# A TensorE order written out by hand for an attention stage, and a tail that transposes over all score banks

## The chip, the cores and the metric

One core of one Trainium2 chip. The metric is the device time of one launch in microseconds (us). The engines that matter here: TensorE (PE, with its weight loads PEld), VectorE (DVE), ScalarE (ACT), GpSimd (POOL), and SyncE (SP), whose queue issues most DMAs.

## What is computed

Two layers of a mixer block over 2048 latent and 256 context tokens, width 1024. Each layer projects its normed input into four branches (attention, convolution, Fourier mixing, spatial gating), gates them and projects them back. The change concerns the attention of each layer and the norm at the end of the convolution branch, which runs beside it. All in float32:

```python
def _attend(q, k, v):                       # 4 heads, 64+32 wide
    scale = 1.0 / math.sqrt(QK_NOPE + QK_ROPE)
    s = jnp.einsum("bqhd,bkhd->bhqk", q, k) * scale
    pr = jax.nn.softmax(s, axis=-1)
    return jnp.einsum("bhqk,bkhd->bqhd", pr, v)

# latent queries read 2048 + 256 keys; context queries (layer 0 only) read 256 keys
# convolution branch: y = silu(layernorm(depthwise_conv(glu)))   then a 256x256 product
# layer: x = x + gate * (concat(attn, conv, four, sgu) * silu(gates)) @ w_out
```

## The kernel before

The kernel is written for a planner: code is emitted in program order, the planner puts each engine's instructions into one fixed order by priority (program order) and by what it reckons to be ready, assigns buffers from pools of a fixed count, and places every wait. So the order on TensorE is fixed before the run, but by the planner and not by the program text.

A layer has three stages: projections (phase A), attention, and the output projection. Attention runs over two **pairs** of heads (`attention`). A pair runs over **jobs** of 256 queries: 8 latent jobs of 18 key tiles each and, in layer 0, one context job of 2 key tiles in second place. A job has four **steps** j (2 heads x 128 queries). The work of a step:

- **Scores** (`score_steps`): five PSUM banks of 512, 512, 512, 512 and 256 keys. A bank is three matmuls (`mm3`, a hi/lo split: L286 to L288). VectorE takes each bank's maximum (L1008), then the row's maximum (L1012); only then ScalarE turns the five banks into `e` tiles by exp (L1017). The pool `s` has 5 banks, so a step's first bank is free again when the step before has had its first exp.
- **Key tiles** of the job before (`av_steps`): four transposes of `e` into a bank of the pool `t` (L1038, 2 banks), copied to `et` by DVE (L1041, letter v) or ACT (L1043, letter a).
- **Products with V** (L1031): two heads, each written once in the code and run as two instructions, so four instructions a key tile, into the one bank `o`. In the code they come two key tiles at a time, at least three behind the transposes (`LAG`, `GRP`).
- **Reciprocals**: four diagonal tiles (POOL L1077), broadcast by matmuls into a `t` bank (L1054), copied by ACT (L1057), multiplied by DVE (L1061) and stored (L1062).
- **Convolution** (`side`): two taps on DVE (L1459) and one half of a norm step (`Conv.tail`): first two transposes of `cac` into a `t` bank (L1492), DVE statistics (L1494), a power on POOL (L292) and the normed tile (L1499); in the next call two transposes back (L1503) and two copies (L1505). There are 18 such tiles in layer 0 and 16 in layer 1.

`PLAN` is the program order of a step: s is a score bank, v or a a key tile. After it comes one `side()`. The last job's key tiles are emitted alone at the end (the **tail**), v and a in turn. Before attention a tiny exp is emitted so that ACT has its table (L1321). K1 (`k1p`) holds the keys of the second pair, loaded in the second job (`half`).

Of the kernel before, what the change touches and what calls it, by code (L numbers as in the profile page):

```python
# [24 lines left out]
P = 128  # L25
# [173 lines left out]
class Kern:  # L199
    def __init__(self, tc, A, outT):  # L200
        self.tc = tc
        self.nc = tc.nc
        self.A = A
        self.outT = outT
        self.n = 0
        self.pse = self.np = self.ap = None
        self.cnt, self.dq, self.every, self.conv = 0, [], None, None
        self.lastp = False


    def nm(self, s):
# [63 lines left out]
    def split(self, src, hi, lo):  # L275
# [2 lines left out]
        b = self.nc.vector.tensor_tensor(lo, src, hi.bitcast(F32), op=ALU.subtract)  # L278
        return a.ins, b.ins

    def mm3(self, out, ks, start=True, stop=True):

        n = len(ks)
        mm = self.nc.tensor.matmul
# [734 lines left out]
        job.es.append(es)  # L1019
        yield  # L1020

    def av_steps(self, p, vt, job):

        nc = self.nc
        dgs = job.dgs

        def product(kt, et):
            g = job.k0 // P + kt
            for q in range(2):
                h = 2 * job.p + q  # L1030
                nc.tensor.matmul(job.o[64 * q:64 * q + 64, 0:256], lhsT=vt[:, g, 64 * h:64 * h + 64],  # L1031
                                 rhs=et[:, 256 * q:256 * q + 256], start=kt == 0, stop=kt == job.nk - 1)

        pend = []
        for kt in range(job.nk):
            ps = self.bank("t")
            for j in range(4):
                nc.tensor.transpose(ps[:, j * P:(j + 1) * P], job.es[j][kt], self.ident)  # L1038
# [5 lines left out]
            if kt == 0:  # L1044
                job.o = self.bank("o")
            pend.append((kt, et))
            if len(pend) >= LAG + GRP:
                for _ in range(GRP):
                    product(*pend.pop(0))
            if kt == min(RBK, job.nk - 1):  # L1050
                rb = self.bank("t")
                for j in (0, 2, 1, 3):
                    q, t = j // 2, j % 2
                    nc.tensor.matmul(rb[64 * q:64 * q + 64, t * P:(t + 1) * P], lhsT=self.ones[:, :64], rhs=dgs[j],  # L1054
                                     start=True, stop=True)
                rs = self.x("co", 256)
                nc.scalar.copy(out=rs, in_=rb[:, 0:256])  # L1057
            if kt == job.nk - 1:
                for e in pend:
                    product(*e)  # L1060
                nc.vector.tensor_tensor(rs, job.o[:, 0:256], rs, op=ALU.mult)  # L1061
                nc.gpsimd.dma_start(out=job.S["att"][job.p * P:(job.p + 1) * P, job.q0:job.q0 + 256], in_=rs)  # L1062
            yield 1


    PLAN = ["vsssssvav", "vassasssvv"]

    def av_queue(self, p, vt):

        nc, job = self.nc, self.avw  # L1070
        rs = self.st()
        nc.vector.reduce_sum(rs[:, 0:4], job.sm[:, :, :5 if job.k0 == 0 else 1], axis=AX.X)
        nc.vector.reciprocal(rs[:, 4:8], rs[:, 0:4])
        job.dgs = []
        for j in range(4):
            dg = self.dg()
            nc.gpsimd.tensor_scalar(dg, self.ident, rs[:, 4 + j:5 + j], None, op0=ALU.mult)  # L1077
            job.dgs.append(dg)
        self.avq.append(self.av_steps(p, vt, job))

    def av_go(self, n=None):

        while self.avq and (n is None or n > 0):
            if next(self.avq[0], None) is None:
                self.avq.pop(0)
            elif n is not None:
                n -= 1

    def attention(self, l, S, p, vt, qpool, pr, keys, side, half, first=None):
# [8 lines left out]
        ahead = list(first or [])  # L1098
        for i, q0 in enumerate(qs):
            job = Job()  # L1100
            job.p, job.q0, job.S = pr, q0, S
            job.k0, klen = (0, NTOK) if q0 < T else (T, C)
            job.nk = klen // P
            job.es, job.sm = [], self.t(p, "sm", [P, 4, 5], bufs=3)
            if i == 0 and not first:
                ahead = [load(0), load(1)]
            qq = ahead.pop(0)
            if i > 0 and i + 1 < len(qs):
                ahead.append(load(i + 1))
            if i == 1:  # L1110
                half()
            for j in range(4):
                sc = self.score_steps(p, job, keys[j // 2], qq[j // 2], (j % 2) * P,
                                      list(FB[j]) if first and i == 0 else [])
                for c in self.PLAN[j % 2] if q0 < T else ("vs", "as")[j % 2]:
                    if c == "s":
                        next(sc, None)
                    else:
                        self.evac = c
                        self.av_go(1)  # L1120
                if not first or i > 0:
                    side()
# [132 lines left out]
    def build(self):  # L1255
        tc, nc, A = self.tc, self.nc, self.A
        with ExitStack() as es:
# [37 lines left out]
            for l in range(L):  # L1295
# [11 lines left out]
                with self.pool(f"V{l}", "right") as vp:  # L1307
# [14 lines left out]
                    with self.pool(f"B{l}", "right") as p, self.pool(f"K1_{l}", "right") as k1p:  # L1322
                        tail = conv.tail(k1p)
                        next(tail)

                        def side():
                            with tc.issue_after(self.red.ins):
                                conv.pump(LATE)
                            return next(tail, True)

                        kn = []
                        self.avq, self.avw, self.ep = [], None, k1p
                        self.attention(l, S, p, vt, k0p, 0, keys, side, lambda: kn.extend(self.load_keys(S, k1p, 1)), [q0, q1])
# [5 lines left out]
                        self.attention(l, S, p, vt, vp, 1, kn, side, lambda: None)  # L1339
                        while not side():  # L1340
                            pass
                        self.av_queue(p, vt)
                        while self.avq:
                            self.av_go(1)
# [7 lines left out]
                with self.pool(f"O{l}", "right") as p, self.pool(f"G{l}", "right") as gp:  # L1352
                    if last:
                        self.np = p
                    blocks = list(range(0, T, 256)) + ([] if last else [T])
                    wpw = self.load_wpw(l, gp, wop)
                    ys = self.out_load(l, 0, S, wpw, gp, wop, ORD1)
                    ws += self.load_wo(l, gp, range(4, 8), wop)
                    for i, t0 in enumerate(blocks):
                        nxt = []  # L1360

                        def ahead():
                            if i + 1 < len(blocks):
                                nxt.extend(self.out_load(l, blocks[i + 1], S, wpw, gp, (p, wop)[i % 2], OUT_ORDER))
# [8 lines left out]
                        self.tick()  # L1373
                    if not last:
                        S = self.scratch(l + 1)
                wo.__exit__(None, None, None)
            self.pse.close()

# [5 lines left out]
class Conv:  # L1384
# [76 lines left out]
    def tail(self, pool):  # L1461
# [19 lines left out]
        for t0 in range(0, end, w):  # L1481
# [6 lines left out]
            for t in range(w // P):  # L1488
                sl = slice(t * P, (t + 1) * P)
                ps = k.bank("t")  # L1490
                for c in range(2):
                    nc.tensor.transpose(ps[:, c * P:(c + 1) * P], acc[c][:, sl], k.ident)  # L1492
# [7 lines left out]
                yield  # L1500
                tr = k.bank("t")
                for c in range(2):
                    nc.tensor.transpose(tr[:, c * P:(c + 1) * P], yn[:, c * P:(c + 1) * P], k.ident)  # L1503
# [20 lines left out]
```

## Time and profile before

| | us |
|---|---|
| median of three runs (2925.22 to 2936.71) | 2926.96 |
| the profiled execution | 2933.03 |
| its span on the core | 2931.3 |
| attention of layer 0, first score to last product with V | 747.8 to 1314.3 |
| attention of layer 1 | 2167.6 to 2711.1 |

The span holds 1.7 us less than the execution, and the profiled execution is 6.1 us above the median of the runs. In a timeline the columns are start, duration, engine, line, operation, tiles and shape, and the count of equal instructions in a row. A matmul's duration includes its pipeline, so what an instruction costs TensorE is read from one start to the next.

### The profile page before, as it was taken

To read this page: it belongs to the slowest core of one execution; us is meant where nothing else is said; L and a number is where in the kernel's file an instruction comes from. 1 tells how busy PE (TensorE), PEld (TensorE's weight loads), DVE (VectorE), ACT (ScalarE), POOL (GpSimd) and SP (SyncE) were. 2 spreads that over 40 slices of the span, in tenths; PEclk is the share of its full clock that TensorE was granted. 3 is DMA by queue.
4 is the path that set the end of the run, shared out by engine and by line. 5 is a ranking of instruction groups with operands and counts; after the bars stand their busy time and mean duration, and the time that the engine had idled before them with its cause. 6 is when DMAs were issued, how large, how long until landed. Compare 5 with 4: busy or idle time off the path is not lost. (4 is left out here: it accounts for less than half of the span.)

```text
span 2931.3 us, 50512 instructions
## 1 busy us (share of the span) xinstructions
PE 2826.8 (96%) x18434; PEld 2425.8 (83%) x18434; DVE 1958.5 (67%) x4301; ACT 1207.0 (41%) x3228; POOL 549.8 (19%) x901
## 2 busy tenths in 40 slices
PE   6999999999899999999999999999989999999998
PEld 4889999999667766769998899998776777776998
DVE  4578498485477777654444695894837777775554
ACT  3432343433344555543223343343434455554432
POOL 1311311421111011012322113114301100111210
PEclk9999999999899999999999999999999999999999
DMA  7465343434611010016543543443543101000653
GB/s 247 138 200 177 107 135 108 144 128 130 182 45 33 25 51 23 21 35 211 178 156 126 164 153 104 135 135 128 172 160 91 35 21 46 17 28 24 183 154 112
DMA packets 222745, 326.75 MB, mean 111 GB/s; under 512 B 33456, under 2 KB 153264, under 8 KB 221728
## 3 DMA queue, kind: packets, MB, share of 16 engines
q1 hardware_dynamic: 194368, 245.51, 27.8%
q0 software_dynamic: 27696, 77.98, 7.7%
q8 instruction: 145, 2.38, 0.4%
q14 instruction: 104, 0.85, 0.1%
q10 hardware_dynamic: 432, 0.04, 0.0%
HBM read 232.30 MB, written 91.10 MB: 110 GB/s over the span
## 5 line engine op out<-in xcount | busy, mean ns | idle before, releaser
L286 PE MATMUL mm<-hh,ring 128*128 128x384 f32 (+1 forms) x1408 | 489.6, 348 | 0.0
L288 PE MATMUL mm<-hh,ring 128*128 128x384 f32 (+1 forms) x1408 | 483.1, 343 | 1.8 <-DVE ring L278 1.7
L1017 ACT ACTIVATE e<-s,st 128x512 f32<-128x512 f32 (+1 forms) x636 | 400.1, 647 | 203.8 <-DVE st L1012 191.6
L1008 DVE TENSOR_REDUCE st<-s 128x1 f32<-128x512 f32 (+1 forms) x636 | 384.0, 630 | 148.8 <-PE s L288 146.7
L287 PE MATMUL mm<-hl,ring 128*128 128x384 f32 (+1 forms) x1408 | 483.2, 343 | 0.0
L1459 DVE SCALAR_TENSOR_TENSOR acc<-win,c_cw,acc 128x384 f32<-128x384 f32 (+5 forms) x780 | 426.9, 570 | 7.5
L1038 PE MATMUL t<-ident,e 128*128 128x128 f32 x2320 | 344.0, 279 | 3.9 <-DVE et L1041 2.6
L1031 PE MATMUL o<-et,v 128*64 128x256 f32 x2320 | 344.6, 392 | 0.0
L1038 PEld LDWEIGHTS t<-ident,e 128*128 128x128 f32 x2320 | 261.5, 142 | 96.4 <-issue 42.4
L1041 DVE COPY et<-t 128x512 f32<-128x512 f32 x377 | 257.9, 686 | 97.5 <-PE t L1038 90.2
L286 PE MATMUL mm<-yh,woh 128*128 128x256 f32 x1040 | 296.9, 285 | 5.6 <-ACT woh L277 3.1
L287 PE MATMUL mm<-yl,woh 128*128 128x256 f32 x1040 | 293.8, 283 | 0.0
L288 PE MATMUL mm<-yh,wol 128*128 128x256 f32 x1040 | 293.4, 282 | 0.2 <-DVE wol L278 0.2
L277 ACT CAST ring<-wst 128x256 fp32r<-128x256 f32 (+2 forms) x480 | 183.5, 418 | 262.2 <-DMA wst<-winC 158.1
L286 PEld LDWEIGHTS mm<-hh,ring 128*128 128x128 f32 x1408 | 266.0, 189 | 19.3 <-issue 9.9
L288 PEld LDWEIGHTS mm<-hh,ring 128*128 128x128 f32 x1408 | 266.1, 189 | 8.6 <-DVE ring L278 2.8
L287 PEld LDWEIGHTS mm<-hl,ring 128*128 128x128 f32 x1408 | 266.3, 189 | 5.9
L1043 ACT COPY et<-t 128x512 f32<-128x512 f32 x203 | 119.2, 588 | 331.2 <-PE t L1038 330.7
L278 DVE TENSOR_TENSOR ring<-wst,ring 128x256 fp32r<-128x256 f32 (+2 forms) x480 | 199.9, 449 | 83.4 <-ACT ring L277 76.9
L1031 PEld LDWEIGHTS o<-et,v 128*64 128x64 f32 x2320 | 153.1, 136 | 98.9 <-issue 52.4
L286 PEld LDWEIGHTS mm<-yh,woh 128*128 128x128 f32 x1040 | 198.3, 191 | 7.1 <-ACT woh L277 3.5
L287 PEld LDWEIGHTS mm<-yl,woh 128*128 128x128 f32 x1040 | 198.3, 191 | 0.3 <-DVE yl L278 0.3
(310 smaller groups left out, 5265.1 us busy)
## 6 DMA issues: line engine op xcount, KB each, us to landing
wst<-winC SPq DMA_DIRECT2D x192, 256.0 KB, 3.1
ast<-wada SPq DMA_DIRECT2D x32, 512.0 KB, 4.7
gt<-g SPq DMA_DIRECT2D x102, 128.0 KB, 3.0
g<-co POOLq DMA_DIRECT2D x60, 192.0 KB, 2.5
wst<-winB SPq DMA_DIRECT2D x24, 384.0 KB, 3.7
x<-xn POOLq DMA_DIRECT2D x72, 128.0 KB, 2.7
ast<-wada SPq DMA_DIRECT2D x8, 1024.0 KB, 8.7
fst<-ft SPq DMA_DIRECT2D x32, 256.0 KB, 3.3
```

Source lines behind the costliest of these rows:

```text
L277: a = self.nc.scalar.copy(out=hi, in_=src)
L278: b = self.nc.vector.tensor_tensor(lo, src, hi.bitcast(F32), op=ALU.subtract)
L286: mm(out, lhsT=lh, rhs=rh, start=start and i == 0, stop=False)
L287: mm(out, lhsT=lh, rhs=rl, start=False, stop=False)
L288: self.last = mm(out, lhsT=ll, rhs=rh, start=False, stop=stop and i == n - 1)
L1008: self.red = nc.vector.reduce_max(mx[:, i:i + 1], ps[:, :w], axis=AX.X)
L1017: nc.scalar.activation(out=e, in_=ps, func=AF.Exp, bias=nb[:, 0:1], accum_out=sm[:, i:i + 1])
L1031: nc.tensor.matmul(job.o[64 * q:64 * q + 64, 0:256], lhsT=vt[:, g, 64 * h:64 * h + 64], rhs=et[:, 256 * q:256 * q + 256], start=kt == 0, s ...
L1038: nc.tensor.transpose(ps[:, j * P:(j + 1) * P], job.es[j][kt], self.ident)
L1041: nc.vector.tensor_copy(et, ps)
L1043: nc.scalar.copy(out=et, in_=ps)
L1459: eng.scalar_tensor_tensor(ac, win[:, t:t + w], v["cw"][:, l, c, t:t + 1], ac, op0=ALU.mult, op1=ALU.add)
```

## The change

- `behind` and `whole` chain every TensorE instruction of attention to the one before it in program order (an edge without a semaphore): scores, key tiles, products, reciprocals and the convolution's transposes. The planner can no longer reorder them.
- A step is now `vnbvsasasss` (j even) or `vnbvsasasass` (j odd): key tile, convolution step (n), **burst** (b), key tile, then score banks and key tiles in turn. A context step is `vnbvs`.
- `av_burst` issues all products of the waiting key tiles but the last one (`LAG` 1), of one job at a time, and behind a job's last key tile the reciprocals, which go into the free half of bank `o`.
- ACT copies 5 of 9 key tiles where it copied 3 of 9.
- Buffers: `e` 21 and 10 for 23 and 9, `et` 8 for 5. Room for them comes from the first block's `y` tiles, which get a pool of their own after attention (`yp`).
- Keys of the second pair are loaded in the fourth job, its first queries in the last job but one.
- Tail: four key tiles (v, a, v, a), then a burst; transposes take turns over one `t` and two `s` pools' banks (`"tsstss"`). A tiny Silu is emitted ahead of it, for ACT's table.

```diff
-EB, EB2, LAG, GRP, ETB, RBK = 23, 9, 3, 2, 5, 4
+EB, EB2, LAG, ETB = 21, 10, 1, 8
+    def whole(self, r):
+        if self.chain is not None:
+            if self.chain:
+                self.behind(r.ins, self.chain[0])
+            self.chain = [r.ins]
+        return r
...
+    def av_burst(self, vt, lag=LAG):
+        nc = self.nc
+        todo = [e for e in self.pend[:max(0, len(self.pend) - lag)] if e[0] is self.pend[0][0]]
+        if not todo:
+            return
+        self.pend = self.pend[len(todo):]
+        job = todo[0][0]
+        if todo[0][1] == 0:
+            job.o = self.bank("o")
+        for _, kt, et in todo:
+            g = job.k0 // P + kt
+            for q in range(2):
+                h = 2 * job.p + q
+                self.whole(nc.tensor.matmul(job.o[64 * q:64 * q + 64, 0:256], lhsT=vt[:, g, 64 * h:64 * h + 64],
+                                            rhs=et[:, 256 * q:256 * q + 256], start=kt == 0, stop=kt == job.nk - 1))
+        if kt < job.nk - 1:
+            return
+        for j in (0, 2, 1, 3):
+            q, t = j // 2, j % 2
+            dg = self.dg()
+            nc.gpsimd.tensor_scalar(dg, self.ident, job.inv[:, 4 + j:5 + j], None, op0=ALU.mult)
+            self.whole(nc.tensor.matmul(job.o[64 * q:64 * q + 64, 256 + t * P:256 + (t + 1) * P], lhsT=self.ones[:, :64],
+                                        rhs=dg, start=True, stop=True))
...
-    PLAN = ["vsssssvav", "vassasssvv"]
+    PLAN = ["vnbvsasasss", "vnbvsasasass"]
...
-                for c in self.PLAN[j % 2] if q0 < T else ("vs", "as")[j % 2]:
+                for c in self.PLAN[j % 2] if q0 < T else "vnbvs":
                     if c == "s":
                         next(sc, None)
+                    elif c == "b":
+                        self.av_burst(vt)
+                    elif c == "n":
+                        if not first or i > 0:
+                            side()
...
+                        nc.scalar.activation(out=self.st()[:, 0:1], in_=self.mhalf[:, 0:1], func=AF.Silu)
+                        self.tb = "tsstss"
                         while self.avq:
-                            self.av_go(1)
-                            self.evac = "v" if self.evac == "a" else "a"
+                            for c in "vava":
+                                self.evac = c
+                                self.av_go()
+                            self.av_burst(vt)
+                        while self.pend:
+                            self.av_burst(vt, 0)
```

## Rows read from the trace of the kernel before

**Rows 1.** The page's first part: busy us and share of each engine.
```profile
PE 2826.8 (96%) x18434; PEld 2425.8 (83%) x18434; DVE 1958.5 (67%) x4301; ACT 1207.0 (41%) x3228; POOL 549.8 (19%) x901
```
**Rows 2.** Windows: both attentions, then a tail; length, busy by engine, PEclk, DMA share.
```profile
747.00:1314.00 567.00, 553.12 (x3542) 395.07 (x3540) 400.56 (x846) 281.17 (x789) 66.02 (x115) 0.98 0.17 49
...
2167.00:2711.00 544.00, 534.23 (x3460) 383.83 (x3458) 395.62 (x818) 274.81 (x769) 56.87 (x98) 0.99 0.16 47
...
1299.00:1313.00 14.00, 14.00 (x112) 9.20 (x111) 4.15 (x6) 4.44 (x9) 0.00 (x0) 1.00 0.05 13
```
**Rows 3.** Timeline, PE: the first and the last run of products with V.
```profile
782.55 1.51 PE L1031 MATMUL o<-et,v 128*64 128x256 f32 x10
...
2709.14 1.95 PE L1031 MATMUL o<-et,v 128*64 128x256 f32 x16
```
**Rows 4.** Timeline, PE, layer 0: key tiles among scores, then among products.
```profile
838.12 0.60 PE L1038 MATMUL t<-ident,e 128*128 128x128 f32 x4
838.47 0.48 PE L288 MATMUL s<-k1h,ql 96*128 96x512 f32 x1
838.79 0.39 PE L286 MATMUL s<-k1h,qh 96*128 96x512 f32 x1
...
841.06 1.08 PE L1031 MATMUL o<-et,v 128*64 128x256 f32 x8
842.08 0.66 PE L1038 MATMUL t<-ident,e 128*128 128x128 f32 x4
842.66 0.65 PE L1031 MATMUL o<-et,v 128*64 128x256 f32 x2
843.24 0.66 PE L1038 MATMUL t<-ident,e 128*128 128x128 f32 x4
843.83 1.08 PE L1031 MATMUL o<-et,v 128*64 128x256 f32 x6
844.83 0.44 PE L1492 MATMUL t<-ident,cac 128*128 128x128 f32 x2
```
**Rows 5.** Timeline, PE, layer 1: a long run of products, a convolution transpose behind it.
```profile
2337.05 1.95 PE L1031 MATMUL o<-et,v 128*64 128x256 f32 x16
2338.93 0.44 PE L1492 MATMUL t<-ident,cac 128*128 128x128 f32 x2
2339.20 0.60 PE L1038 MATMUL t<-ident,e 128*128 128x128 f32 x4
```
**Rows 6.** The chain in order of time: the same run in successive jobs (start, us).
```profile
2302.93 1.88 PE o L1031 x16
2337.12 1.88 PE o L1031 x16
...
2498.40 1.88 PE o L1031 x16
2529.77 1.88 PE o L1031 x16
```
**Rows 7.** Timeline, layer 0: first instruction behind a step's scores; the step's first exp.
```profile
1276.36 0.60 PE L1038 MATMUL t<-ident,e 128*128 128x128 f32 x4
...
1277.92 0.69 ACT L1017 ACTIVATE e<-s,st 128x512 f32<-128x512 f32 x1 [2.55 <-DVE st L1012]
```
**Rows 8.** Timeline, layer 1: a convolution tile's transposes, and its normed tile on DVE.
```profile
2677.33 0.38 PE L1492 MATMUL t<-ident,cac 128*128 128x128 f32 x2
...
2679.84 0.54 DVE L1499 TENSOR_SCALAR yn<-t,st,st 128x256 f32<-128x256 f32 x1
```
**Rows 9.** Groups by line, attention of layer 0: key tiles copied by DVE and ACT.
```profile
L1041 DVE COPY et<-t 128x512 f32<-128x512 f32 x189 | 129.1, 686 | 54.1 <-PE t L1038 51.7 <-ACT et L1043 1.9
...
L1043 ACT COPY et<-t 128x512 f32<-128x512 f32 x103 | 60.4, 588 | 166.1 <-PE t L1038 165.9
```
**Rows 10.** Timeline, PE: the first convolution transpose of layer 0 and its wait.
```profile
773.35 0.47 PE L1492 MATMUL t<-ident,cac 128*128 128x128 f32 x1 [0.45 <-DMA cac<-dw]
```
**Rows 11.** The line of the early exp: engine, count, durations in ns, first and last start.
```profile
L1321 ACT ACT_TABLE_LOAD  x2: 1283/1283/1283, 632.9 to 2085.1; - x2
```

More of the change, by code (lines that the diff above doesn't have):

```diff
@@ L208, in __init__ @@
         self.lastp = False
+        self.chain = None
     def nm(self, s):
@@ L279, in split, with behind, mm @@
         return a.ins, b.ins
+    def behind(self, ins, prev):
+        self.tc.add_manual_dep(ins, prev.name, mybir.DependencyInfo(mybir.DependencyClass.NoSync, mybir.DependencyReason.DATA),
+                               reason="order of TensorE")
+    def whole(self, r):
[4 more added lines that the diff above has]
+        return r
     def mm3(self, out, ks, start=True, stop=True):
         n = len(ks)
-        mm = self.nc.tensor.matmul
+        def mm(*a, **kw):
+            return self.whole(self.nc.tensor.matmul(*a, **kw))
         for i, (lh, ll, rh, rl) in enumerate(ks):
@@ L1020, in score_steps, with av_steps @@
         yield
-    def av_steps(self, p, vt, job):
+    def av_steps(self, p, job):
         nc = self.nc
[L1025 to L1034, printed above, removed]
         for kt in range(job.nk):
-            ps = self.bank("t")
+            self.tb = self.tb[1:] + self.tb[:1]
+            ps = self.bank(self.tb[0])
             for j in range(4):
-                nc.tensor.transpose(ps[:, j * P:(j + 1) * P], job.es[j][kt], self.ident)
+                self.whole(nc.tensor.transpose(ps[:, j * P:(j + 1) * P], job.es[j][kt], self.ident))
             et = self.t(self.ep, "et", [P, 512], bufs=ETB)
@@ L1043, in av_steps @@
                 nc.scalar.copy(out=et, in_=ps)
[L1044 to L1062, printed above, removed]
-            yield 1
-    PLAN = ["vsssssvav", "vassasssvv"]
+            self.pend.append((job, kt, et))
+            yield 1
+    def av_burst(self, vt, lag=LAG):
[21 more added lines that the diff above has]
+                                        rhs=dg, start=True, stop=True))
+        rs = self.x("co", 256)
+        nc.scalar.copy(out=rs, in_=job.o[:, 256:512])
+        nc.vector.tensor_tensor(rs, job.o[:, 0:256], rs, op=ALU.mult)
+        nc.gpsimd.dma_start(out=job.S["att"][job.p * P:(job.p + 1) * P, job.q0:job.q0 + 256], in_=rs)
@@ L1068, in av_queue @@
+    PLAN = ["vnbvsasasss", "vnbvsasasass"]
     def av_queue(self, p, vt):
         nc, job = self.nc, self.avw
[L1071 to L1089, printed above, removed]
+        job.inv = self.st()
+        nc.vector.reduce_sum(job.inv[:, 0:4], job.sm[:, :, :5 if job.k0 == 0 else 1], axis=AX.X)
+        nc.vector.reciprocal(job.inv[:, 4:8], job.inv[:, 0:4])
+        self.avq.append(self.av_steps(p, job))
@@ L1091, in attention, with av_go @@
+    def av_go(self):
+        while self.avq and next(self.avq[0], None) is None:
+            self.avq.pop(0)
+    def attention(self, l, S, p, vt, qpool, pr, keys, side, half, first=None, pre=None):
         qs = list(range(0, T, 256))
@@ L1096, in load @@
             return [self.load_q(S, qpool, 2 * pr + q, qs[i]) for q in range(2)]
-        ahead = list(first or [])
+        ahead = list(first or pre)
         for i, q0 in enumerate(qs):
@@ L1104, in attention @@
             job.es, job.sm = [], self.t(p, "sm", [P, 4, 5], bufs=3)
-            if i == 0 and not first:
-                ahead = [load(0), load(1)]
             qq = ahead.pop(0)
-            if i > 0 and i + 1 < len(qs):
+            if (i > 0 or not first) and i + 1 < len(qs):
                 ahead.append(load(i + 1))
-            if i == 1:
-                half()
+            if i == len(qs) - 2:
+                half(1)
+            if i == 3:
+                half(0)
             for j in range(4):
@@ L1331, in build, with half @@
                         kn = []
-                        self.avq, self.avw, self.ep = [], None, k1p
-                        self.attention(l, S, p, vt, k0p, 0, keys, side, lambda: kn.extend(self.load_keys(S, k1p, 1)), [q0, q1])
+                        self.avq, self.avw, self.pend, self.ep = [], None, [], k1p
+                        self.chain, self.tb = [], "t"
+                        pre = []
+                        def half(n):
+                            if n == 0:
+                                kn.extend(self.load_keys(S, k1p, 1))
+                            else:
+                                pre.append([self.load_q(S, vp, 2 + q, 0) for q in range(2)])
+                        self.attention(l, S, p, vt, k0p, 0, keys, side, half, [q0, q1])
                         k0.__exit__(None, None, None)
@@ L1338, in build @@
                             ws = self.load_wo(l, wop, range(4), wop)
-                        self.attention(l, S, p, vt, vp, 1, kn, side, lambda: None)
+                        self.attention(l, S, p, vt, vp, 1, kn, side, lambda n: None, None, pre)
                         while not side():
@@ L1342, in build @@
                         self.av_queue(p, vt)
+                        nc.scalar.activation(out=self.st()[:, 0:1], in_=self.mhalf[:, 0:1], func=AF.Silu)
+                        self.tb = "tsstss"
                         while self.avq:
-                            self.av_go(1)
-                            self.evac = "v" if self.evac == "a" else "a"
+                            for c in "vava":
+                                self.evac = c
+                                self.av_go()
+                            self.av_burst(vt)
+                        while self.pend:
+                            self.av_burst(vt, 0)
+                        self.chain = None
                 self.psum(pj=2, mm=3, hold=3)
@@ L1355, in build @@
                     blocks = list(range(0, T, 256)) + ([] if last else [T])
+                    yx = self.pool(f"Y{l}", "left")
+                    yp = yx.__enter__()
                     wpw = self.load_wpw(l, gp, wop)
-                    ys = self.out_load(l, 0, S, wpw, gp, wop, ORD1)
+                    ys = self.out_load(l, 0, S, wpw, gp, yp, ORD1)
                     ws += self.load_wo(l, gp, range(4, 8), wop)
@@ L1363, in ahead @@
                             if i + 1 < len(blocks):
-                                nxt.extend(self.out_load(l, blocks[i + 1], S, wpw, gp, (p, wop)[i % 2], OUT_ORDER))
+                                nxt.extend(self.out_load(l, blocks[i + 1], S, wpw, gp, (p, yp)[i % 2], OUT_ORDER))
                         self.out_block(l, t0, xs, x1src, ws, ys, p, OUT_ORDER if i else ORD1, ahead)
@@ L1375, in build @@
                         S = self.scratch(l + 1)
+                    yx.__exit__(None, None, None)
                 wo.__exit__(None, None, None)
@@ L1491, in tail @@
                 for c in range(2):
-                    nc.tensor.transpose(ps[:, c * P:(c + 1) * P], acc[c][:, sl], k.ident)
+                    k.whole(nc.tensor.transpose(ps[:, c * P:(c + 1) * P], acc[c][:, sl], k.ident))
                 bn, mv, r = k.st(), k.st(), k.st()
@@ L1502, in tail @@
                 for c in range(2):
-                    nc.tensor.transpose(tr[:, c * P:(c + 1) * P], yn[:, c * P:(c + 1) * P], k.ident)
+                    k.whole(nc.tensor.transpose(tr[:, c * P:(c + 1) * P], yn[:, c * P:(c + 1) * P], k.ident))
                 for c in range(2):
```

2 lines of the change are left out of this document (removed).

## The prediction

> **What bounds the kernel now.** First the page's busy table: TensorE works 96% of the span, VectorE 67%, ScalarE 41% [rows 1]. [...] The change takes no work from it, so the gain has to come from what a matmul costs in its place in the order. That is read in timelines of PE, from one start to the next; the chain of waits in order of time then gives the period of a job, and the timelines of DVE, ACT and POOL what the new order would have to wait for.
>
> **What a run of products costs.** Four transposes between score matmuls take 838.47 - 838.12 = 0.35 us, and the next score matmul 0.32 for its usual 0.23, so 0.44 in all; the same four between two runs of products take 0.58 and 0.59 [rows 4]. A run of 8 products takes 842.08 - 841.06 = 1.02, a run of 16 takes 1.88 [rows 4, 5]: 0.43 a key tile (four products) and 0.16 once. So each separate run costs 0.16 + 0.15 = 0.31 us whatever its length; I use 0.30. A run that cuts a key tile in half costs more: 2 products take 0.58 and 6 take 1.00, for 0.37 and 0.80 by that line [rows 4], so 0.2 each; the two heads' products, which go to different columns, then don't overlap.
>
> Counted in the timeline of PE from the first run to the last [rows 3], there are 166 + 157 = 323 runs in the two layers, 112 of them not whole key tiles. Read off the code, the written order has one burst a step and 6 or 7 in a tail: 72 + 64 = 136 runs, none cut. The saving is 187 x 0.30 = 56 us and 112 x 0.2 = 22 us, together **78 us**. A test by periods: the run of 16 comes again after 2337.12 - 2302.93 = 34.2 us in jobs with 11 runs, 6 of them cut, and four convolution steps, and after 31.4 in jobs with 8 whole runs and none [rows 6]. By my prices the difference is 3 x 0.30 + 6 x 0.2 + 4 x 0.27 [rows 5] = 3.2, against 2.8 measured. The model holds within some 10%. A job afterwards, with 4 runs, should take 31.4 - 4 x 0.30 = 30.2 us, and 31.2 with convolution steps.
>
> Twice as many runs of scores (209 for 122 a layer) cost nothing by rows 4: 0.44 us for four transposes there is no more than among themselves.
>
> **What the fixed order adds.** From here on PE waits wherever the next instruction in the text isn't ready, and everything behind it waits too.
>
> *First bank of a step.* Behind a step's scores PE now has key tile, convolution step, burst of 4 or 5, key tile: about 0.53 + 1.88 + 0.41 = 2.8 us, 3.25 with 5, and 0.27 more with a convolution step [rows 4, 5]. The bank is free after the maxima, the first exp and its hand-over: 1277.92 - 1276.36 + 0.69 = 2.25 us [rows 7], and about 0.55 more where DVE is held up by a norm. The cover is 0 to 0.9 us longer, so I take 3 us in all for about 124 steps, with bounds 0 and 25. In layer 0, two steps behind the context jobs have no key tiles left to cover with: 2 x 1.6 = 3 us.
>
> *Banks of transposes.* A convolution tile holds one of two `t` banks from its transposes to its normed tile: 2679.84 + 0.54 - 2677.33 = 3.05 us [rows 8]. In the new step, burst, key tile and a score bank lie between, 3.2 to 3.7 us; but a key tile's copy (0.69 [rows 9]) and two taps now stand on DVE at the same place. A wait of 0 to 1.8 us; I take 0.4, near the lower end since rows 8 already contain DVE's queue. 34 x 0.4 = 14 us, bounds 0 and 61.
>
> *Start.* The first convolution tile lands behind V, at 773.35 in layer 0 [rows 10]; PE had been filling that time with scores of the second job. Written ahead of these scores, it holds them. I take 3 us a layer, 6 in all (bounds 0, and 12 if nothing else is saved there), and 2 us for the context job, where the two halves of a norm step follow closely.
>
> *Silu ahead of the tail.* Its like, the exp of L1321, was run at 632.9 and 2085.1 by the planner, 115 and 82 us ahead of attention [rows 11], so the table had to be loaded again. The Silu has no input to wait for either: I expect it in mid-attention, with two loads of 1.28 us there and none saved at the end. ACT has room for that. 2 us in all; bounds: 2.6 gained, 5 lost.
>
> *What hides the rest.* ACT takes 5 of 9 copies instead of 3: about 58 more in layer 0, 34 us on 281 of 567 busy; DVE sheds 40 us of 401 [rows 2, 9]: neither becomes the bound. The bursts wait for no copy, as the last key tile is left out. 21 `e` buffers: 16 belong to a job and 4 come with each step, and four fall free in each step: 20. Moving 24 key loads out of the second job frees SP's queue for the convolution's and the queries' loads; with the reordering this takes back some waits of the start: 5 us gained, bounds 0 and 10. The reciprocals' bank copy stays on ACT; their diagonals on POOL have had their input for a job's length. The `y` tiles in their own pool: nothing, they are written only behind attention. The tail goes by the prices above; with seven banks it waits for no copy.
>
> **The sum.** 78 - 3 - 3 - 14 - 6 - 2 - 2 + 5 = 53 us. From the profiled execution, 2933.0 - 53 = 2880; this one is 6.1 above the median, so **2874 us** against 2926.96, 1.8% faster.
>
> **Rivals.**
> *Nothing waits:* the transposes' banks and the first banks cost nothing (+17) and the start and Silu come out at their good ends (+8): 78 us, 2849. For it: PE waits 2% of attention now. Against: the planner had filled gaps that the text no longer can.
> *The norm's bank takes it back:* DVE's queue puts taps and a copy ahead of the statistics, each of 34 tiles holds PE by 1.6 us instead of 0.4: 41 us lost, 2915. For it: two banks only, and key tile, norm, key tile now come in a row. Against: rows 8.
> *Slower, no cover:* each step's first score bank comes late. If a copy on DVE (0.69) stands ahead of the maxima, and a copy on ACT (0.59) and half an exp ahead of the first exp, the bank comes 1.6 to 1.8 us later than rows 7 show, 1.0 beyond the cover, in 124 steps: 2874 + 124 = 2998. It decides from about 0.9 us of lateness in every step, where the gain is gone. Against: the maxima are earlier in the text than those copies, and ACT's last copy of a step ends before the exps of that step can start.
> *It doesn't do what it says:* the runs don't merge, or PE's cost lies in the number of key tiles and not of runs: 2927. Against: rows 6.
> [...]
>
> **How the numbers follow.** Forecast 0.56 (its own range 2855 to 2900); nothing waits 0.13; norm's bank 0.12; slower 0.10; doesn't do it 0.06; clock 0.03. The range 2842 to 2916 holds the first three and leaves out less than 2 in 10; its lower end is 85 us of gain, its upper the norm's bank. About 0.5%, 15 us, is what a measurement of this kernel can tell from no change, so faster means under 2912: forecast, nothing waits, and a share of the norm's bank, 0.74; slower 0.10; the same 0.16.
>
> **What would show it.** Right: 4 runs of products a job, periods near 30 to 31.5 us, attention of about 540 and 518 us, idle PE of some 40 to 50 us in both. First banks: PE waiting for ACT's exp at the first score matmul of a step. Norm's bank: PE waiting for DVE L1499 or a copy at the first key tile behind a score bank. Start: a PE gap up to 773 and to about 2194. Silu: a table load in mid-attention. The prediction is wrong if the runs merge and the periods stay, which would mean that a run's 0.30 us isn't the run's.

## The result, and the profile after

The changed kernel takes 2862.34 us (median of four runs, 2857.63 to 2863.22) against 2929.36 us for the kernel before in the same comparison: a ratio of 0.976, 95% interval 0.974 to 0.978. The forecast was 2874 us, with a range of 2842 to 2916. The profiled execution took 2863.22 us, 69.8 less than that of before (2933.03).

First the page's busy table, then the windows of both attentions and of a stretch of the tail (columns as in [rows 1] and [rows 2], which they answer):

```profile
PE 2744.2 (96%) x18434; PEld 2420.6 (85%) x18434; DVE 1893.4 (66%) x4193; ACT 1268.9 (44%) x3338; POOL 551.6 (19%) x901
```

```profile
744.00:1272.50 528.50, 509.70 (x3542) 389.87 (x3540) 369.67 (x798) 309.25 (x838) 66.02 (x115) 0.98 0.17 51
2131.50:2641.50 510.00, 496.96 (x3459) 383.26 (x3457) 360.31 (x758) 308.27 (x829) 57.47 (x98) 0.98 0.17 50
1248.00:1262.00 14.00, 13.77 (x121) 10.07 (x122) 4.74 (x9) 7.85 (x19) 3.99 (x7) 1.00 0.08 20
```

The share of PE is 96% as before, so the page's first line alone hides the gain. The windows show it: the same matmuls keep PE busy for 509.70 + 496.96 = 1006.7 us where it was 553.12 + 534.23 = 1087.4 [rows 2]. **That is 80.7 us less work in the same work.** Idle PE in the two windows went the other way, from 23.7 to 18.8 + 13.0 = 31.8 us. The windows are rounded a little outwards: from first score to last product with V the attentions became 74.0 us shorter, and the rest of the kernel about 4 us longer, 3 less ahead of the first attention and 7 more between the two. That stretch takes 850 to 867 us in the kernels below, whose edits lie inside attention, so I put nothing down to it.

A regular job without convolution steps, in the timeline of PE of layer 1 (the runs of products, and the reciprocals that close a job):

```profile
2432.03 2.38 PE L1068 MATMUL o<-et,v 128*64 128x256 f32 x20
...
2439.38 1.95 PE L1068 MATMUL o<-et,v 128*64 128x256 f32 x16
2441.16 0.61 PE L1076 MATMUL o<-dg,ones 128*64 128x128 f32 x8
...
2447.19 2.38 PE L1068 MATMUL o<-et,v 128*64 128x256 f32 x20
...
2454.54 1.95 PE L1068 MATMUL o<-et,v 128*64 128x256 f32 x16
...
2461.93 2.38 PE L1068 MATMUL o<-et,v 128*64 128x256 f32 x20
...
2469.28 1.95 PE L1068 MATMUL o<-et,v 128*64 128x256 f32 x16
2471.05 0.61 PE L1076 MATMUL o<-dg,ones 128*64 128x128 f32 x8
```

Four runs a job of 5, 4, 5 and 4 whole key tiles, and 2471.05 - 2441.16 = 29.9 us from one job's close to the next, for 31.4 with eight whole runs in [rows 6]: 1.5 us for four runs fewer, 0.37 each. A job with convolution steps takes 31.0 for 34.2:

```profile
2196.93 0.61 PE L1076 MATMUL o<-dg,ones 128*64 128x128 f32 x8
...
2225.88 0.38 PE L1536 MATMUL t<-ident,yn 128*128 128x128 f32 x2
2226.19 1.95 PE L1068 MATMUL o<-et,v 128*64 128x256 f32 x16
2227.97 0.61 PE L1076 MATMUL o<-dg,ones 128*64 128x128 f32 x8
```

What PE waited for in the attention of layer 0 (us in total, times, longest), all waits but the smallest:

```profile
PE t L1525 <- DMA cac<-dw: 7.2, 1, 7.2
PE s L1044 <- ACT e L1032: 1.8, 1, 1.8
PE t L1044 <- DVE yn L1532: 1.7, 1, 1.7
PE s L298 <- DMA qh<-qrh: 1.5, 1, 1.5
PE s L298 <- ACT e L1032: 1.2, 1, 1.2
```

Most of what is lost stands at the start, above all one wait of 7.2 us for the first convolution tile's rows (5.1 in layer 1), where [rows 10] had 0.45. The line `s L1044` is the tail's first transposes, which take a bank that the last step's scores still hold, 1.8 us in each layer. Neither the first score banks of a step nor the norm's bank makes a wait that comes back job after job.

### The profile page after: what moved, and what is told of

Its sections match the earlier page's. It is cut to its first block, busy times and chain, and to the rows that moved or that the text cites. A ratio compares the mean times of both kernels' runs of the same rounds, so it can differ in the third digit from the quotient of the medians.

```text
span 2861.4 us, 50568 instructions
## 1 busy us (share of the span) xinstructions
PE 2744.2 (96%) x18434; PEld 2420.6 (85%) x18434; DVE 1893.4 (66%) x4193; ACT 1268.9 (44%) x3338; POOL 551.6 (19%) x901
## 5 line engine op out<-in xcount | busy, mean ns | idle before, releaser
L298 PE MATMUL mm<-hh,ring 128*128 128x384 f32 (+1 forms) x2816 | 761.6, 346 | 2.1 <-DVE ring L278 2.1
L298 PEld LDWEIGHTS mm<-hh,ring 128*128 128x128 f32 x2816 | 516.3, 190 | 27.6 <-issue 10.7
L1023 DVE TENSOR_REDUCE st<-s 128x1 f32<-128x512 f32 (+1 forms) x636 | 391.1, 632 | 152.3 <-PE s L298 150.6
L1044 PE MATMUL t<-ident,e 128*128 128x128 f32 x2200 | 341.0, 278 | 3.7 <-DVE yn L1532 1.7
L1044 PEld LDWEIGHTS t<-ident,e 128*128 128x128 f32 x2200 | 260.4, 141 | 90.6 <-issue 29.7
L1068 PE MATMUL o<-et,v 128*64 128x256 f32 x2320 | 281.3, 386 | 0.0
L298 PE MATMUL mm<-ring,hh 128*128 128x384 f32 (+2 forms) x1152 | 275.1, 326 | 5.1 <-ACT ring L277 4.1
L1047 DVE COPY et<-t 128x512 f32<-128x512 f32 x255 | 174.6, 685 | 105.1 <-PE t L1044 103.1
L1049 ACT COPY et<-t 128x512 f32<-128x512 f32 x295 | 174.1, 592 | 91.3 <-PE t L1044 89.9
L298 PEld LDWEIGHTS mm<-ring,hh 128*128 128x128 f32 x1152 | 201.2, 193 | 14.6 <-ACT ring L277 6.2
L298 PEld LDWEIGHTS mm<-yh,wol 128*128 128x128 f32 x1040 | 197.0, 189 | 2.8 <-DVE wol L278 2.8
```

What stands on the lines that cost most here:

```text
L298: return self.whole(self.nc.tensor.matmul(*a, **kw))
L1023: self.red = nc.vector.reduce_max(mx[:, i:i + 1], ps[:, :w], axis=AX.X)
L1044: self.whole(nc.tensor.transpose(ps[:, j * P:(j + 1) * P], job.es[j][kt], self.ident))
L1068: self.whole(nc.tensor.matmul(job.o[64 * q:64 * q + 64, 0:256], lhsT=vt[:, g, 64 * h:64 * h + 64], rhs=et[:, 256 * q:256 * q + 256], start ...
```

## The experiments

All times are medians; a ratio is to the kernel before in the same comparison, and the changed kernel's is 0.976. "Attention" is the sum of both layers from first score to last product with V: 1110.0 before, 1036.0 changed.

### Is it the chain, or the order in the text?

```diff
-                        self.chain, self.tb = [], "t"
+                        self.chain, self.tb = None, "t"
```

> The changed kernel with the chain on TensorE left off: same program text, the planner may reorder again. Its order then has 156 runs of products with V instead of 136, and 11 key tiles are cut in two. Theory (a run of products costs 0.30 us wherever it stands, a cut run 0.2 more): 20 x 0.30 + 22 x 0.2 = 10 us slower than the changed kernel, about 2872. Rival (the written order as such brings the gain, since it keeps every engine to one rhythm): most of the 67 us come back, 2910 or more.

Measured: 2858.91 us, ratio 0.9743 (0.9726 to 0.976). The chain earns nothing by itself. Given the new program text the planner makes 156 runs of products (16 of them cut) where the chain has 136, with the same periods of 29.9 and 30.8 us. Its busy PE in the attentions is 10.7 us higher, about what 20 more runs and 16 cuts cost by the prices found below (9.0), and its idle PE 18.1 us for 31.8: it places ready work in front of the late convolution tile and ahead of the tail's first transposes. The gain lies in the new text: bursts of a step's products and their place. That was not what I expected.

```diff
-EB, EB2, LAG, GRP, ETB, RBK = 23, 9, 3, 2, 5, 4
+EB, EB2, LAG, GRP, ETB, RBK = 23, 9, 1, 4, 5, 4
```

The kernel before, with the products four key tiles at a time and one behind the transposes:

> The kernel before with products four key tiles at a time, one behind the transposes, still in the planner's order: 251 runs instead of 321, 45 key tiles cut instead of 61. Theory: 70 x 0.30 + 32 x 0.2 = 27 us faster than before, about 2902. Rival (only the written order brings the gain): 2929, no change.

Measured: 2912.7 us, ratio 0.9931 (0.9911 to 0.9951), 21.8 below its companion. It has 253 runs for 323, 90 of them cut for 112. So 70 runs fewer are worth 0.31 us each, less if part is put down to the cuts; by the prices found below 28 us would have come. Busy PE in the attentions fell by 24.0 and idle PE rose by 2.3; what the other 4 are stays open. Longer groups alone are under a third of the gain: the planner still leaves 253 runs.

### What does a run cost?

```diff
-    PLAN = ["vnbvsasasss", "vnbvsasasass"]
+    PLAN = ["vnbvsasabsss", "vnbvsasabsass"]
```

> The changed kernel with a second burst behind the second key tile among the scores of each step: 251 runs of products with V instead of 136, none cut, everything else the same. Theory: 115 x 0.30 = 35 us slower than the changed kernel, about 2897. Rival (the gain is in whole key tiles and in waits, the number of runs is free): 2862, no change. If a burst has to wait for its last copy, more than 35 us, with PE waiting for ACT's copy.

Measured: 2973.4 us, ratio 1.0135 (1.0117 to 1.0154): 111 us above the changed kernel, not 35. It has 251 runs, 115 more, yet a job takes 34.0 us without convolution steps, 4.1 more. The timeline shows where more than half of that comes from. The mid-step burst leaves one or two key tiles for the burst at the head of a step, and the step's first score matmul then stands on a bank whose exp isn't done:

```profile
2592.36 0.61 PE L1076 MATMUL o<-dg,ones 128*64 128x128 f32 x8
2592.90 0.66 PE L1044 MATMUL t<-ident,e 128*128 128x128 f32 x4
2594.15 0.50 PE L298 MATMUL s<-k0h,qh 96*128 96x512 f32 x1 [0.59 <-ACT e L1032]
```

From the last transpose's start to the score matmul's, the places where one follows the other take 2.85 us a job for 0.40 in the changed kernel, some 2.5 more; the other 1.6 us belong to four more runs. Idle PE in both attentions rose from 31.8 to 69.4 us. This kernel moved two things at once, the number of runs and the cover ahead of a bank, so the next one was meant to move the number alone:

```diff
-    PLAN = ["vnbvsasasss", "vnbvsasasass"]
+    PLAN = ["vnbvbsasasss", "vnbvbsasasass"]
```

> The changed kernel with one more burst letter behind the second V key tile of a step: a step's run of four key tiles of products is cut once, by one key tile's transposes, and stays at the head of the step. Nothing else is moved, so no score bank should be waited for. Runs of products go from 136 to about 260. My theory (the run is the price, 0.30 us each as forecast, 0.42 us as the kernel with two bursts gives it without its waits): 2862 + 124 x 0.30 to 0.42 = 2899 to 2914, with no new waits of TensorE in the attention. Rival (a run in itself costs nothing; what the kernel with two bursts lost was its waits for the exponentials in ScalarE): 2862 to 2866.

Measured: 2999.05 us, ratio 1.0223 (1.0196 to 1.025). "No new waits" was wrong. Two successive jobs' closes, in layer 1:

```profile
2512.62 0.60 PE L1076 MATMUL o<-dg,ones 128*64 128x128 f32 x8
2516.32 0.65 PE L1068 MATMUL o<-et,v 128*64 128x256 f32 x4 [2.51 <-DVE co L1080]
...
2546.48 0.60 PE L1076 MATMUL o<-dg,ones 128*64 128x128 f32 x8
2550.18 0.65 PE L1068 MATMUL o<-et,v 128*64 128x256 f32 x4 [2.51 <-DVE co L1080]
```

The second burst letter of a closing step starts the next job's products at once, and there is one bank `o`: PE waits 2.51 us until the closed job has been multiplied out of it. In the changed kernel a step has one burst, of one job, so a whole step lies between. This wait comes 28 times, 70 us in all. What is left gives the price of a run: 2546.48 - 2512.62 = 33.86 us a job, 3.97 more than the changed kernel's 29.89, less 2.51, is 1.46 us for 4 more whole runs, **0.37 us each**, with 0.23 us from one score matmul to the next in both jobs (the granted clock is 1.00 in the changed kernel's). It is the price that [rows 6] gave against the changed kernel's job, so the rival of a free run is out, and the forecast's 0.30 was a little low. By that price 187 fewer runs make 69 of the 80.7 us, and some 11 are left for the 112 cuts, 0.1 each where the forecast had 0.2. The jobs with convolution steps agree: 34.2 - 31.0 = 3.2 us for 7 runs and 6 cuts fewer, of which the runs are 2.6. No kernel here changes the cuts alone, and the change's other parts (ACT's share of the copies, the buffers, the later key loads) were not tried by themselves; by these prices they have no part in the busy time.

### What covers the first score bank, and the norm's bank?

The burst behind the first score bank instead of ahead of it:

```diff
-    PLAN = ["vnbvsasasss", "vnbvsasasass"]
+    PLAN = ["vnsbvsasass", "vnsbvsasasas"]
```

> The changed kernel with the burst one score bank later and one fewer score bank at the end of the step (V, norm, bank, burst, V, ...). What stands at the step's end between the last V copy's key tile and its products gets one bank shorter, and the bank that the next key tile's exponential fills is asked for earlier. Theory of the cover (the last banks hide the VectorE and ScalarE work behind a step): 1.5 us of waiting at each of about 120 steps, 2862 + 180 = about 3040. Rival (the order of banks within a step does not matter, as the exponentials run ahead): 2860 to 2880.

A single run: 3137.18 us. The rival's 20 us are far away, and the theory's 180 are too few. PE's main wait in layer 1, a step of it in the timeline, and the windows of both attentions:

```profile
PE s L298 <- ACT e L1032: 82.1, 55, 1.8
```

```profile
2525.73 0.60 PE L1044 MATMUL t<-ident,e 128*128 128x128 f32 x4
2527.69 0.50 PE L298 MATMUL s<-k0h,qh 96*128 96x512 f32 x1 [1.35 <-ACT e L1032]
```

```profile
745.00:1409.50 664.50, 562.71 (x3543) 404.06 (x3541) 373.97 (x798) 314.80 (x839) 65.12 (x115) 0.93 0.14 41
2264.00:2914.20 650.20, 551.44 (x3460) 396.78 (x3458) 362.04 (x758) 314.18 (x828) 57.05 (x98) 0.92 0.14 40
```

Idle PE is 201 us, 169 more than changed. Busy PE rose too, by 107 us with equally many runs of products, and the mean granted clock fell from 0.98 to 0.93 and 0.92. By these means the share not granted comes to 0.07 x 664.5 + 0.08 x 650.2 = 98.5 us, for 0.02 x 528.5 + 0.02 x 510.0 = 20.8 in the changed kernel; that would be 78 of the 107 us (an estimate). That is the forecast's slower rival made real. In the changed kernel only the burst ahead of the bank stands between it and this.

The norm step behind the burst:

```diff
-    PLAN = ["vnbvsasasss", "vnbvsasasass"]
+    PLAN = ["vbnvsasasss", "vbnvsasasass"]
```

> The changed kernel with the convolution's norm step behind the burst (V, burst, norm, V) instead of ahead of it. The half's VectorE work of 1.9 us then stands on the bank `t` with only one key tile of transposes between, and no products as cover. Theory (the product burst is what hides the norm's bank): TensorE waits 1.2 to 1.9 us at each of 34 halves, 2862 + 41 to 65 = 2903 to 2927. Rival (the bank is free anyway, because VectorE's queue delays nothing): within 5 us of 2862.

Measured: 2868.56 us, ratio 0.9777 (0.9754 to 0.98), which can't be told from the changed kernel. By the traces attention is 8.0 us longer; jobs with convolution steps take 31.9 for 31.0, in delays of about 0.2 us, read from start to start, for key tiles' copies on DVE behind the statistics. The theory of 41 to 65 us falls: products as cover aren't what keeps the norm's bank harmless. What does is seen in a kernel that was meant for the start, with the norm steps one step later:

```diff
-                        if not first or i > 0:
+                        if not first or i > 1 or i == 1 and j > 0:
                             side()
```

> The changed kernel with the first convolution step one step later, so that the second job's first scores no longer stand behind the transpose that waits for its load. Theory: the gaps of PE ahead of that transpose (7.3 us in layer 0, 5.2 in layer 1) go, and the scores fill them: 5 to 10 us faster, about 2854. Rival (the scores of that step would wait for the exps of the first job anyway, or the clock stays low): within 2 us of 2862.

Measured: 2883.08 us, ratio 0.9822 (0.9804 to 0.9841): 20 us slower than the changed kernel, where 5 to 10 faster were expected. By the traces its attention is 9.3 us longer; the other 10 of the profiled executions lie outside it, 7 of them between the attentions, where no edit was made, and stay unexplained. In both attentions PE waits 15.0 us for normed tiles:

```profile
PE t L1044 <- DVE yn L1532: 9.2, 9, 1.7
PE t L1044 <- DVE yn L1532: 5.8, 4, 1.6
```

At seven jobs' closes it stands for 1.6 to 1.7 us each, and DVE and POOL show why:

```profile
2212.64 0.63 PE L1044 MATMUL t<-ident,e 128*128 128x128 f32 x4 [1.63 <-DVE yn L1532]
```

```profile
2211.95 0.55 DVE L1532 TENSOR_SCALAR yn<-t,st,st 128x256 f32<-128x256 f32 x1 [2.27 <-POOL st L307]
```

```profile
2209.60 1.77 POOL L1075 TENSOR_SCALAR dg<-ident,st 128x128 f32<-128x128 f32 x3 [14.98 <-PE o L1076]
2211.34 0.57 POOL L307 TENSOR_TENSOR st<-st,mhalf 128x1 f32<-128x1 f32 x1
2211.90 0.61 POOL L1075 TENSOR_SCALAR dg<-ident,st 128x128 f32<-128x128 f32 x1
```

Four diagonals take POOL 0.59 us each. They are the next job's: they get their buffers when the closed job's have been multiplied (L1076), and so come at a close, a job ahead of their use. The norm's power (0.57) stands behind three of them; DVE waits 2.27 us for it and holds the `t` bank. One step of shift brought the first halves into closing steps, thirteen of them. In the changed kernel thirteen closes meet a *second* half, which needs no power: in the fence of the job with convolution steps, `L1536` (transposes of `yn`) stands ahead of the run whose end is `L1076`. Two closes meet a first half:

```profile
1073.69 1.77 POOL L1075 TENSOR_SCALAR dg<-ident,st 128x128 f32<-128x128 f32 x3 [3.73 <-DVE st L1528]
1075.44 0.57 POOL L307 TENSOR_TENSOR st<-st,mhalf 128x1 f32<-128x1 f32 x1
...
1105.78 0.55 POOL L307 TENSOR_TENSOR st<-st,mhalf 128x1 f32<-128x1 f32 x1 [14.67 <-DVE st L1529]
1106.32 2.36 POOL L1075 TENSOR_SCALAR dg<-ident,st 128x128 f32<-128x128 f32 x4
```

At the first, three diagonals stand ahead of the power, and PE has its one wait of 1.7 us for a normed tile. At the second the power comes first, and PE doesn't wait; four closes of the kernel with the late norm are like that too. So the wait that the forecast priced at 0 to 1.8 us is real. The step that a half falls in makes it possible, and the place of the power in POOL's order, which the planner fixes, decides it.

### The tail

Without the Silu ahead of the tail:

```diff
-                        nc.scalar.activation(out=self.st()[:, 0:1], in_=self.mhalf[:, 0:1], func=AF.Silu)
```

> The changed kernel without the one-column Silu that loads ScalarE's table ahead of the tail. The table of Silu is then loaded at the end of each attention, as in the kernel before. Theory: the end of each attention grows by the 0.6 us that the gap shrank, and the low granted clock of 6.8 us behind it comes back in each layer, at most 3.4 us each: 2862 + 1 to 8 = 2863 to 2870. Rival (the load in the tail delays the tail's exponentials by its 1.3 us, and taking it out gives that back): 2858 to 2862.

Measured: 2861.99 us, ratio 0.9742 (0.9718 to 0.9766): no difference. In the trace the load of 1.28 us stands behind layer 0's attention, and PE's gap there is 3.71 us where the changed kernel has 1.95. The matmuls behind it start 0.22 us apart, for 0.12 in the changed kernel, whose granted clock is 1.00 there; one trace doesn't show that this part is the Silu's. It is worth a few us at most, below what the runs can tell.

The tail's transposes over the two `t` banks alone:

```diff
-                        self.tb = "tsstss"
```

> The changed kernel with the tail's transposes over the two banks `t` alone, as in the kernel before. What the tail over all score banks is worth: the theory says each tail loses its wait of 1.8 us for a score bank but waits for the copies of VectorE and ScalarE at each third key tile, 0 to 2 us per layer either way: 2860 to 2866, the last part of each attention 52.8 and 54.9 us within 2. Rival (the two banks hold up each key tile by 0.2 us or more): 3 to 6 us more in each layer, 2868 to 2874.

A single run: 2861.34 us; from the last score matmul to the last product the two layers take 26.8 us each for 25.8 and 27.3. The 1.8 us at the tail's start go, and five waits of 0.35 to 0.53 us for copies come in each tail. The tail over all score banks gains nothing that this run can tell.

### Can the start be had back?

The norm steps two steps later, so that each half keeps its kind of step, and a burst ahead of the tail's transposes:

```diff
-                        if not first or i > 0:
+                        if not first or i > 1 or i == 1 and j > 1:
                             side()
...
                         self.tb = "tsstss"
+                        self.av_burst(vt)
```

> The changed kernel with the convolution's first norm step two steps later (the same parity of halves and steps, where one step of shift gave 1.8 us of waiting at a job's close), and with one burst of products ahead of the tail's transposes. Theory: TensorE's wait of 7.3 and 5.2 us for the first rows of `cac` shrinks to under 2 us in each layer, no half meets the four `dg` of a job's close, and the wait of 1.8 us at the start of each tail is covered by the burst: 2862 - 6 - 3 = about 2853. Rival (the waits at the start only move to the keys and queries that arrive late, as they did in the kernel with one step of shift): 2860 to 2865 with the tail's part alone.

Measured: 2843.81 us, ratio 0.9691 (0.9669 to 0.9714). The wait for the first convolution tile is 1.98 us in layer 0 and gone in layer 1, no power stands behind a job's diagonals, and the `s` wait at the tail's start is gone:

```profile
774.49 0.69 PE L1526 MATMUL t<-ident,cac 128*128 128x128 f32 x2 [1.98 <-DMA cac<-dw]
```

By the traces attention is 14.7 us shorter than the changed kernel's, 3.5 of them the two `s` waits, where one step of shift made it 9.3 longer. A new wait of 2.85 us stands in layer 1's tail, for a norm step that now falls there. Then the tail's burst without the chain, the norm steps where they were:

```diff
-                        self.chain, self.tb = [], "t"
+                        self.chain, self.tb = None, "t"
...
                         self.tb = "tsstss"
+                        self.av_burst(vt)
```

> The changed kernel without the chain that fixes TensorE's order (the planner places the instructions of the same text), and with one burst of products ahead of the tail's transposes. Theory: as without the chain (2859), less 1.8 us in each layer where the tail's first transposes waited for the bank of the last scores: 2855. Rival (the planner has the burst there already, so nothing is left to win): 2859.

Measured: 2857.37 us, ratio 0.9741 (0.9721 to 0.9761), the same as without the burst (0.9743), as the rival said: the planner had filled that place. Last, all three edits:

> No chain, the first norm step two steps later, and a burst ahead of the tail's transposes. Theory: the planner fills the start already, so the later norm step adds nothing to the kernel without the chain and with the burst: 2855. Rival (the start's waits are for data, and each is worth its time): 2850.

Measured: 2839.8 us, ratio 0.9673 (0.9654 to 0.9691), against 0.9741 without the later norm steps. The theory (2855) falls: the planner had not filled the start. Of the 13.8 us that the later norm steps take from the attentions, 6.1 are idle PE and 7.7 busy time; the mean granted clock of the profiled executions is 0.985 for 0.980. The windows of both attentions of this kernel:

```profile
746.00:1263.00 517.00, 509.23 (x3541) 386.66 (x3540) 368.81 (x798) 308.55 (x839) 66.13 (x115) 0.99 0.18 52
2119.50:2620.00 500.50, 495.99 (x3460) 381.89 (x3458) 359.79 (x758) 307.66 (x828) 56.97 (x98) 0.98 0.18 52
```

Idle PE is 7.8 + 4.5 = 12.3 us for 31.8, at the same busy time. This is the best of the kernels, some 22 us below the changed one and 96 below its companion of before. Against the version with the chain its interval touches, so those two can't be told apart.

## Why the prediction was right, step by step

- **A run of products, 78 us.** Right in kind and size: PE's busy time in the attentions fell by 80.7 us. The counts of 136 runs, 72 + 64, none cut, and 4 a job, came as read from the code. The split was off: a whole run costs 0.37 us, not 0.30, and a cut about 0.1, not 0.2. The forecast's own test by periods pointed there: it gave 3.2 for 2.8 measured, and with these prices it gives 2.8. The total fits as well as it does by luck: 13 us more by the runs and 11 less by the cuts nearly cancel. Periods of 29.9 and 31.0 stand against the forecast 30.2 and 31.2.
- **More alternation of scores and transposes, nothing.** Right: layer 1 has 209 runs of scores for 121, and a run of products has the same price, 0.37 us, whether a job's changes from transposes to scores go from 4 to 14 (from the kernel before to the changed one) or from 14 to 10 (the second burst letter).
- **First bank of a step, 3 us; two uncovered steps, 3 us.** Right. In layer 1 PE waits 1.1 us in all for an exp at a score bank, and layer 0's two steps behind the context jobs cost 1.5 (a query load) and 1.2 us (an exp).
- **Norm's bank, 14 us.** This is the term that was mis-sized. There is one such wait, 1.7 us in the job behind the context job, and none in the other jobs. I looked for cover on PE and for DVE's queue; what holds the bank too long is POOL's queue, and only in a closing step. I had put POOL aside with "their diagonals on POOL have had their input for a job's length". In the trace they start about 1 us behind their input (L1092), at the close before, and what matters is that they can stand ahead of the norm's power. That the planner mostly had the second half at a close was luck: with the norm one step later PE waited 15.0 us for it.
- **Start, 6 us.** The mechanism was right and the size too small: PE waits 7.2 + 5.1 = 12.3 us for the first convolution tiles, at the bound of 12. Two steps' delay takes most of it away. The waits for exps that the start had before (about 16 us in both layers) have largely gone, so the idle time grew by 8.1 us in all.
- **Silu, 2 us lost.** Wrong. The table was not loaded in mid-attention but in the tail:

```profile
L1366 ACT ACT_TABLE_LOAD  x2: 1283/1283/1283, 1251.7 to 2620.3; - x2
```

  I reasoned from [rows 11] that an activation without inputs is hoisted. This one stayed near its place in the text, and no second load was paid. It costs nothing and, by the kernel without it, gains nothing that can be measured.
- **What hides the rest.** Right: ACT takes 144 + 8 copies in layer 0 where it took 103, 49 more for the forecast 58, and has 309 us of 528 busy. The tail waits for no copy, as forecast, but 1.8 us in each layer for a bank of the last scores, which the sum lacks.
- **The tail's clock.** The forecast gave the clock 0.03. The granted clock in the stretch of layer 0's tail is 1.00, as in [rows 2], and the tail's first four key tiles, 16 transposes in a row, take 1250.35 - 1248.22 = 2.13 us there. In layer 1 the same 16 take 2618.98 - 2615.43 = 3.55 us, at a granted clock of 0.51; the rest of that tail stands at 1.00. Both tails have the row of transposes and a wait of 1.8 us ahead of it, so these alone don't make the difference, and no run shows what does. In the kernel with all three edits, which has no such wait, the granted clock from 1255.0 to 1262.0, in layer 0's tail, is 1.00.
- **The sum.** Forecast 53 us on the profiled executions, measured 69.8. Idle PE grew by 8 us where the terms made it 23, most of that the norm's; the runs gave 3 more and Silu's 2 were not lost; about 4 went outside the attentions, where the sum had nothing: 53 + 15 + 3 + 2 - 4 = 69. Idle PE came to 31.8 us, below the 40 to 50 forecast.

The rival that nothing waits (2849) came nearer in its terms than I gave it credit for: its norm's bank was right, its start wasn't. With the start mended, the kernel with all three edits passes it.

## What to carry to other kernels

Read an order's worth from the busy time of the same instructions in the same window, not from idle time: here 80.7 us lay in how often TensorE changed between products and other work, at a share of 96% on both sides. Where two fixed rhythms meet (halves of a norm step, steps of a job), look at what stands together on the least busy engine too: one step of shift made attention 9 us longer, and two, with a burst ahead of the tail, 15 shorter. And before fixing an order by a chain, try the same program text without it: here the planner did as well.

## What the runs showed of the hardware

- A run of products between other matmuls cost 0.37 us of TensorE beyond its products (33.86 us a job for 29.89, less a wait of 2.51, for four more runs; granted clock 1.00 in the job of 29.89), while more changes between transposes and score matmuls, 14 a job for 4, cost nothing that a period shows.
- With the burst behind the first score bank, short waits that came back cost more than their length: with 55 waits for exps in layer 1's attention, 82.1 us in all and 1.8 at the longest (idle PE 98.8 us there, 101.8 in layer 0), the attentions' mean granted clock fell from 0.98 to 0.93 and 0.92, and busy time for the same matmuls rose by 107 us on top of 169 us of waiting. With one wait of 2.51 us a job it was 0.95 and 0.96.
- With the norm one step later, a 128 x 128 multiply took POOL 0.59 us, and three of them ahead of a one-column power (0.57) were enough to stop TensorE, two engines further on, for 1.63 us.
